# A two-layer diffusion backbone in fp32 on one core: another hand-written order for its first stage

## Chip, cores and metric

The kernel runs on one core of one Trainium2 chip. The metric is device time in microseconds, the median of several executions; lower is better. Input layouts are prepared on the host and are not timed.

## What is computed

Two layers work on 256 context tokens and 256 latent tokens of width 1024. Each layer is a SwiGLU FFN (width 2816), a token mixer, and a second FFN, all wrapped in RMS norms whose shift, scale and gate come from a conditioning vector (one vector for the latent tokens, one for the context). For the change only the first FFN's entry counts:

```
mod_l = silu(c) @ w_mod[l] + b_mod[l]        # 9 vectors of 1024; mod_c from c_ctx
h  = rms_norm(x, norm_pre) * (1 + scale) + shift
g, u = split(h @ w_in, 2)
x  = x + 0.5 * gate * rms_norm((silu(g) * u) @ w_out, norm_post)
```

## The kernel before

Activations lie transposed: `x` is 128 partitions by 8 tiles of 128 channels by 512 tokens (context, then latent). Every product of the FFN is made of three fp32r products: weights and activations are each split into a rounded part (`hi`, `hh`) and a rest (`lo`, `hl`), and hi·hh, hi·hl and lo·hh are summed. `split` (line 168) makes the parts of a weight in two halves, the cast on ScalarE (L173), the subtraction on VectorE (L174); a weight unit is one 512 KB load into one of 4 staging buffers (`raw`), giving 128 output columns.

The first stage has a long chain of its own: `hh` and `hl` for a pair of channel tiles need the RMS statistics of all of `x`, and the shift and scale of that pair. Shift and scale are a quarter of a small matrix product: `quarter_load` (L977) brings 2 MB of `w_mod` in 8 loads, `quarter_rows` (four fp32 products of 512 columns each, in four 32-row strips of one bank, issued as 8 instructions) multiplies them with `cs` = silu(c), `quarter_end` copies the rows on ScalarE (L989), transposes them back with small products (tile `pc`) and finishes the vectors on VectorE (L203, L206). The rest of the modulation is not made this way but by `mod_tile`, which sums on VectorE (L196) against `cb`, a broadcast silu(c); these sums run as a stream beside other work.

Inside `first_units` (L1040 and on) the order of SP (which issues the loads), TensorE, VectorE and ScalarE is written by hand: each engine executes its part of the steps in the order of the string `STEPS` (L63). The letters, with a number n:

- `x`: load pair n of `x`. `a`: squares of pair n on ScalarE (L1055, L1058), chained adds on VectorE (L1059). `t`: statistics: products with ones on TensorE, scaling on VectorE (L1069), power -1/2 on GpSimd (L241). `y`: transpose and broadcast of the norm (L1080), copied to SBUF as `rb` by ScalarE (L1081).
- `c`: silu of the conditioning into `cs` (L1018) and the selector `pick` (L1020).
- `q`, `r`, `s`, `f`: loads, first rows, second rows and end of quarter n; quarter n gives the vectors of pair n.
- `u`: load of unit n. `w`: its split.
- `h`: pair n of `hh` and `hl`: scaling by `rb` on VectorE (L1086), `hh` by ScalarE (L1091), the unrounded copy by VectorE for the pair's first tile (L1095) and by ScalarE for its second (L1093), the difference `hl` on VectorE (L1097).
- `*n`: all products that are possible for channel tiles k < n, in the order of k first and unit second. A unit's products keep one PSUM bank over all k.
- `d`, `e`: load and silu of `cb`. `z`, `l`: constants of the mixer.

Six units (0 to 5) go through this stage, 144 products of 512 columns; unit 6 and all after it go through the ordinary path, in which loads, splits and products are ordered by a planner. `product` (L1046) issues the three products of one unit and channel tile:

```
hi, lo = got["w%d" % u]
for j, (w, h) in enumerate(((hi, hh), (hi, hl), (lo, hh))):
    pe.matmul(bank[u], lhsT=w[:, k, :], rhs=h[:, k, :], ...)
```

All matmuls that go through the helper `Products.matmul` stand at L113 in the profile.

Of the kernel before, what the change touches and what calls it, by code (L numbers as in the profile page):

```python
# [8 lines left out]
F32 = mybir.dt.float32  # L9
# [3 lines left out]
OP = mybir.AluOpType  # L13

P = 128
D = 1024
KT = D // P
SEQ = 256
T = 2 * SEQ
# [40 lines left out]

STEPS = ("x1 x3 a1 x0 x2 u1 a3 u0 c0 a0 q0 q1 a2 w0 t0 r0 w1 y0 s0 f0 u2 u4 u3 r1 h0 q2 s1 u5 *2 w2 *2 w4 f1 *2 w3 *2 h1 "  # L63
         "r2 s2 *3 q3 f2 *4 r3 w5 h2 d0 z0 s3 *2 f3 e0 h3 *3 l0 *8")
F_ACT = "vavavava"
MANUAL0 = {mybir.EngineType.SP, mybir.EngineType.PE, mybir.EngineType.DVE, mybir.EngineType.Activation}

# [14 lines left out]
def backbone(ctx: ExitStack, tc: tile.TileContext, xT, vecs, crow, w_mod, w_in, w_out, w_mi, w_mo, w_lru, w_cm, b_cm, lam, w_last, out):  # L82
    nc = tc.nc
    ve, sc, gp, te = nc.vector, nc.scalar, nc.gpsimd, nc.tensor
# [4 lines left out]
    hp = ctx.enter_context(tc.tile_pool(name="hp", bufs=3))  # L89
# [6 lines left out]
    def nm(s):  # L96
        cnt[0] += 1
        return f"{s}_{cnt[0]}"

    def tt_(dt=F32, shape=(P, T)):  # L100
        return tp.tile(list(shape), dt, tag="t", name=nm("t"), bufs=NT)

    def pbank():
        return ps.tile([P, 512], F32, tag="mm", name=nm("mm"))
# [26 lines left out]
    vec = const.tile([P, NVEC], F32, name="vec")  # L131
    nc.sync.dma_start(vec, vecs)
    x = const.tile([P, KT, T], F32, name="x")
    hh = const.tile([P, KT, T], F32R, name="hh")
    hl = const.tile([P, KT, T], F32R, name="hl")

    def V(name, i, n=1):
        o = _OFF[name] + i
        return vec[:, o:o + n]

    ident = const.tile([P, P], F32, name="ident")
# [93 lines left out]
    def mcol(l, v, m, s):  # L235
        return modv[l][:, v, m, s:s + 1]


    def rsqrt(ms, n):
        v = sp.tile([P, n], F32, tag="rs", name=nm("rs"), bufs=4)  # L240
        gp.tensor_tensor(v, ms, power[:, :n], op=OP.pow)  # L241
        return v
# [762 lines left out]
    def halves_sum(v, m, raws):  # L1005
        sums = sp.tile([P, 2, 2], F32, tag="sums", name=nm("sums"), bufs=2)
        for h in range(2):
            for s in range(2):
                ve.scalar_tensor_tensor(junk[:, 0:512], raws[h], 1.0, cb[:, s, 512 * h:512 * h + 512],
                                        op0=OP.mult, op1=OP.mult, accum_out=sums[:, h, s:s + 1])  # L1010
        part = modv[0][:, v, m, :]
        ve.scalar_tensor_tensor(part, sums[:, 0], V("b_mod", v * KT + m), sums[:, 1], op0=OP.add, op1=OP.add)
        if v == 1:
            ve.tensor_scalar(part, part, 1.0, V("norm_pre", m), op0=OP.add, op1=OP.mult)
# [25 lines left out]
    def first_units(evac):  # L1040
        got, bank = {}, {}
        units = 1 + max(int(e[1]) for e in STEPS.split() if e[0] == "u")
        todo = [(k, u) for k in range(KT) for u in range(units)]
        acc, rb = tt_(), tt_()

        def product(k, u):  # L1046
            if k == 0:
                bank[u] = pbank()
            hi, lo = got["w%d" % u]
            for j, (w, h) in enumerate(((hi, hh), (hi, hl), (lo, hh))):  # L1050
                pe.matmul(bank[u], lhsT=w[:, k, :], rhs=h[:, k, :], start=(k == 0 and j == 0), stop=(k == KT - 1 and j == 2))

        def squares(m):
            if not summed:
                sc.activation(acc, x[:, m], AF.Square)  # L1055
            else:
                sq = tt_()
                sc.activation(sq, x[:, m], AF.Square)  # L1058
                ve.tensor_tensor(acc, acc, sq, op=OP.add)  # L1059
            summed.append(m)  # L1060

        summed, dgs = [], []

        def statistics():
            st = ps_st.tile([P, 4, 2], F32, tag="st", name=nm("st"))
            for tt in range(4):
                pe.matmul(st[:, tt, :], lhsT=acc[:, tt * P:(tt + 1) * P], rhs=ones[:, 0:2], start=tt == 0, stop=tt == 3)
            ms0 = const.tile([P, 4], F32, name="ms0")
            ve.tensor_scalar(ms0, st[:, :, 0], 1.0 / D, EPS, op0=OP.mult, op1=OP.add)  # L1069
            r = rsqrt(ms0, 4)  # L1070
            for s in range(2):
                msq[s] = ms0[:, 2 * s:2 * s + 2]
                dgs.append(r[:, 2 * s:2 * s + 2])

        def scales():
            p = ps_st.tile([P, T], F32, tag="st", name=nm("rb"))
            for s in range(2):
                for tt in range(2):
                    a = SEGS[s][0] + tt * P
                    te.transpose(p[:, a:a + P], dgs[s][:, tt:tt + 1].to_broadcast([P, P]), ident)  # L1080
            sc.copy(rb, p)  # L1081

        def first_h(ms):
            tmps = {m: hp.tile([P, T], F32, tag="sg", name=nm("tmp"), bufs=2) for m in ms}
            for m in ms:
                ve.tensor_tensor(tmps[m], x[:, m], rb, op=OP.mult)  # L1086
            for m in ms:
                for s in range(2):
                    a, b = SEGS[s]
                    A, B = mcol(0, 1, m, s), mcol(0, 0, m, s)  # L1090
                    sc.activation(hh[:, m, a:b], tmps[m][:, a:b], AF.Identity, scale=A, bias=B)  # L1091
                    if F_ACT[m] == "a":
                        sc.activation(tmps[m][:, a:b], tmps[m][:, a:b], AF.Identity, scale=A, bias=B)  # L1093
                    else:
                        ve.tensor_scalar(tmps[m][:, a:b], tmps[m][:, a:b], A, B, op0=OP.mult, op1=OP.add)  # L1095
            for m in ms:
                ve.tensor_tensor(hl[:, m], tmps[m], hh[:, m].bitcast(F32), op=OP.subtract)  # L1097

        raws = {}

        for what in STEPS.split():
            c, n = what[0], int(what[1])
            got[what] = True
            if c == "x":
                nc.sync.dma_start(x[:, 2 * n:2 * n + 2], xT[:, 2 * n:2 * n + 2])
            elif c == "a":
                for m in (2 * n, 2 * n + 1):
                    squares(m)
            elif c == "t":
                statistics()  # L1110
            elif c == "y":
                scales()
            elif c == "c":
                conditioning()
            elif c == "d":
                for s in range(2):
                    row = crow[:, s]
                    nc.sync.dma_start(cb[:, s], bass.AP(tensor=row.tensor, offset=row.offset, ap=[[0, P], [1, D]]))
            elif c == "e":
                for s in range(2):  # L1120
                    sc.activation(cb[:, s], cb[:, s], AF.Silu)
            elif c == "u":
                raws[what] = wp.tile([P, KT, P], F32, tag="raw", name=nm("raw"), bufs=NRAW)
                nc.sync.dma_start(raws[what], w_in[0, 0, n])
            elif c == "w":
                got[what] = [wp.tile([P, KT, P], F32R, tag=t, name=nm(t), bufs=NSPL) for t in ("hi", "lo")]
                for a in (0, 4):
                    split(raws["u%d" % n][:, a:a + 4], *(t[:, a:a + 4] for t in got[what]))
            elif c == "q":
                quarter_load(n)  # L1130
            elif c == "r":
                quarter_rows(n, 0)
            elif c == "s":
                quarter_rows(n, 4)
            elif c == "f":
                quarter_end(n)
            elif c in "vb":
                raws[what] = halves_load("bv".index(c), n)
            elif c in "VB":
                halves_sum("BV".index(c), n, raws[what.lower()])  # L1140
            elif c == "h":
                first_h((2 * n, 2 * n + 1))
            elif c == "z":
                mixer_consts(0)
                nc.sync.dma_start(lamt, lam)
            elif c == "l":
                decays()
            else:
                for k, u in list(todo):
                    if k < n and "h%d" % (k // 2) in got and "w%d" % u in got and (k - 1, u) not in todo:  # L1150
                        todo.remove((k, u))
                        product(k, u)
        assert not todo
        for j in range(units // 2):
            evac(j, bank[2 * j], bank[2 * j + 1], 0, T)
        return units // 2
# [24 lines left out]
def _layout(i):  # L1181
# [18 lines left out]
    w_mod = np.ascontiguousarray(wm.transpose(0, 2, 3, 4, 1)).reshape(L, 9, KT, P, D)  # L1200
    for q in (int(e[1]) for e in STEPS.split() if e[0] == "q"):
        rows = wm[0, :, 1::-1, 2 * q:2 * q + 2].reshape(2, 2, 2, P, 512).transpose(0, 1, 3, 2, 4)
# [38 lines left out]
```

## Time and profile before

| | us |
|---|---|
| median of 3 runs | 1646.81 (1646.08 to 1649.19) |
| the profiled execution, its time | 1645.51 |
| the profiled execution, its span | 1643.7 |

The profile is one execution. Times are microseconds from the span's start unless marked ns. PE is TensorE, PEld its weight loads, DVE VectorE, ACT ScalarE, POOL GpSimd, SPq the queue of the engine that issues the loads. A row names the line, the engine, the operation, and output <- input by the program's names; xN counts instructions that stand merged in one row. The chain of waits is followed back from the last instruction, at each step to what released it. Matmuls overlap, so their durations add up to more than the distance between their starts.

### The profile page before, as it was taken

To read this page: it belongs to the slowest core of one execution; us is meant where nothing else is said; L and a number is where in the kernel's file an instruction comes from. 1 tells how busy PE (TensorE), PEld (TensorE's weight loads), DVE (VectorE), ACT (ScalarE), POOL (GpSimd) and SP (SyncE) were. 2 spreads that over 40 slices of the span, in tenths; PEclk is the share of its full clock that TensorE was granted. 3 is DMA by queue.
4 is the path that set the end of the run, shared out by engine and by line. 5 is a ranking of instruction groups with operands and counts; after the bars stand their busy time and mean duration, and the time that the engine had idled before them with its cause. 6 is when DMAs were issued, how large, how long until landed. Compare 5 with 4: busy or idle time off the path is not lost.

```text
span 1643.7 us, 23402 instructions
## 1 busy us (share of the span) xinstructions
PE 1614.8 (98%) x8832; PEld 1372.6 (84%) x8832; DVE 1165.1 (71%) x2183; ACT 735.8 (45%) x1378; POOL 120.0 (7%) x166
## 2 busy tenths in 40 slices
PE   6999999999999999999999999999999999999998
PEld 3788888889977998888888998888888998789997
DVE  4799898548789777866763887767432888875554
ACT  5523322244697662332233562322222579764543
POOL 0000000005000500000000410000000410000000
PEclk9999999999999999999999999999999999989999
DMA  9568677431323225655542226655422316145552
GB/s 372 181 218 258 204 234 225 142 120 48 103 71 119 78 96 186 219 166 170 183 160 87 93 66 193 222 161 171 136 92 88 103 64 217 53 137 196 181 192 78
DMA packets 73906, 249.97 MB, mean 152 GB/s; under 512 B 8384, under 2 KB 10048, under 8 KB 73792
## 3 DMA queue, kind: packets, MB, share of 16 engines
q1 hardware_dynamic: 73216, 247.94, 46.0%
q8 instruction: 69, 1.13, 0.3%
q10 hardware_dynamic: 576, 0.52, 0.1%
q14 instruction: 45, 0.37, 0.1%
HBM read 247.39 MB, written 1.05 MB: 151 GB/s over the span
## 4 chain that ended last, share of the span: by engine, by line
PE 89%; DVE 6%; ACT 3%; issue 1%; DMA 1%; POOL 0%; SPq 0%; POOLq 0%; DVEq 0%; ACTq 0%
PE mm L113 87%; PE st L113 1%; DVE x L271 1%; PE mod L113 1%; DVE sq L394 1%; DVE t L703 0%; DVE z L270 0%; DVE tmp L262 0%; ACT hi L173 0%; DMA x<-in_xT 0%; DVE t L397 0%; POOL rs L241 0%; DVE lo L174 0%; PE pc L113 0%; DVE t L332 0%
## 5 line engine op out<-in xcount | busy, mean ns | idle before, releaser
L173 ACT CAST hi<-raw 128x512 fp32r<-128x512 f32 (+1 forms) x596 | 343.3, 610 | 673.3 <-PE mm L113 476.2
L113 PE MATMUL mm<-hh,hi 128*128 128x512 f32 (+1 forms) x1840 | 627.0, 349 | 1.2 <-ACT hh L263 1.1
L113 PE MATMUL mm<-hl,hi 128*128 128x512 f32 (+1 forms) x1840 | 623.7, 346 | 0.5 <-DVE hl L256 0.5
L174 DVE TENSOR_TENSOR lo<-raw,hi 128x512 fp32r<-128x512 f32 (+1 forms) x596 | 387.2, 679 | 156.1 <-ACT hi L173 153.0
L113 PE MATMUL mm<-hh,lo 128*128 128x512 f32 (+1 forms) x1840 | 467.8, 346 | 0.0
L113 PEld LDWEIGHTS mm<-hh,hi 128*128 128x128 f32 x1840 | 346.9, 189 | 53.7 <-ACT hh L1091 3.3
L113 PEld LDWEIGHTS mm<-hl,hi 128*128 128x128 f32 x1840 | 347.1, 189 | 49.3 <-issue 1.2
L196 DVE SCALAR_TENSOR_TENSOR junk<-raw,cb 128x1024 bf16<-128x1024 f32 x256 | 312.8, 1222 | 77.2 <-DMA raw<-in_w_mod 73.7
L113 PEld LDWEIGHTS mm<-hh,lo 128*128 128x128 f32 x1840 | 326.1, 189 | 47.3
L113 PE MATMUL mm<-t,hi 128*128 128x512 f32 (+1 forms) x1056 | 240.6, 367 | 0.0
L113 PEld LDWEIGHTS mm<-t,hi 128*128 128x128 f32 x1056 | 182.8, 188 | 35.7 <-issue 0.2
L397 POOL TENSOR_TENSOR t<-t,sq 128x256 f32<-128x256 f32 x112 | 94.1, 855 | 712.3 <-ACT sq L391 702.4
L113 PE MATMUL mm<-t,lo 128*128 128x512 f32 (+1 forms) x528 | 131.5, 367 | 0.0
L113 PEld LDWEIGHTS mm<-t,lo 128*128 128x128 f32 x528 | 92.5, 188 | 17.7
L480 DVE TENSOR_TENSOR sg<-sg,mm 128x512 f32<-128x512 f32 (+1 forms) x72 | 45.9, 639 | 76.7 <-PE mm L113 76.7
L113 PE MATMUL mm<-t,hh 128*128 128x256 f32 x512 | 71.2, 281 | 0.0
L113 PEld LDWEIGHTS mm<-t,hh 128*128 128x128 f32 x512 | 65.7, 188 | 0.5
L173 ACT CAST t<-sg 128x512 fp32r<-128x512 f32 (+1 forms) x94 | 50.6, 541 | 34.3 <-DVE sg L480 31.2
L174 DVE TENSOR_TENSOR t<-sg,t 128x512 fp32r<-128x512 f32 (+1 forms) x94 | 55.2, 588 | 1.1 <-ACT t L173 1.1
L113 PE MATMUL mm<-hi,t 128*128 128x512 f32 x176 | 55.1, 394 | 0.0
L332 DVE TENSOR_TENSOR t<-t,mm 128x256 f32<-128x256 f32 (+1 forms) x66 | 35.4, 536 | 27.3 <-PE mm L113 27.1
L263 ACT ACTIVATE hh<-tmp,modv 128x256 fp32r<-128x256 f32 x72 | 42.4, 596 | 23.6 <-DVE tmp L262 23.3
(177 smaller groups left out, 1209.1 us busy)
## 6 DMA issues: line engine op xcount, KB each, us to landing
raw<-in_w_in SPq DMA_DIRECT2D x176, 512.0 KB, 3.5
raw<-in_w_mod SPq DMA_DIRECT2D x128, 512.0 KB, 4.2
raw<-in_w_out SPq DMA_DIRECT2D x48, 512.0 KB, 3.3
raw<-in_w_mi SPq DMA_DIRECT2D x36, 512.0 KB, 4.1
raw<-in_w_last SPq DMA_DIRECT2D x22, 512.0 KB, 3.3
raw<-in_w_out SPq DMA_DIRECT2D x24, 384.0 KB, 3.7
t<-in_w_mod SPq DMA_DIRECT2D x32, 256.0 KB, 5.8
raw<-in_w_mo SPq DMA_DIRECT2D x8, 512.0 KB, 3.9
```

Of the source, the lines that this page charges most:

```text
L113: te.matmul(dst, lhsT=lhsT, rhs=rhs, start=start, stop=stop)
L173: sc.copy(hi, src)
L174: ve.tensor_tensor(lo, src, hi.bitcast(F32), op=OP.subtract)
L196: ve.scalar_tensor_tensor(junk, raw.rearrange("p k c -> p (k c)"), 1.0, cb[:, s], op0=OP.mult, op1=OP.mult, accum_out=modv[l][:, v, m, s:s ...
L263: sc.activation(hh[:, m, a:b], tmp, AF.Identity, scale=A, bias=B)
L271: ve.scalar_tensor_tensor(x[:, m, a:b], z, mcol(l, 3 * i + 2, m, s), x[:, m, a:b], op0=OP.mult, op1=OP.add)
L332: ve.tensor_tensor(y[m][:, a:b], y[m][:, a:b], p[:, :b - a], op=OP.add)
L394: ve.scalar_tensor_tensor(q[2], y, G, x[:, m, a:b], op0=OP.mult, op1=OP.mult)
L397: (gp if JACC[c] == "g" else ve).tensor_tensor(acc[c], acc[c], q[c], op=OP.add)
L480: ve.tensor_tensor(sg[:, :b - a], sg[:, :b - a], pu[:, :b - a], op=OP.mult)
```

## The change

The string of steps is replaced. `c0` comes first. All of quarter 0 is loaded ahead of the units, then units 1, 0, 2 and 4, quarter 1 and unit 3. A new step `n` (`first_n`) takes the scaling by `rb` out of `h`; it is called before `h` of the same pair. A new step `k` (`fill`) issues n fp32 products of 128x128 by 256 columns into a bank that nobody reads: `k2` ahead of `f0`, `k4` behind it, `k2` ahead of `f1`. The split of unit 0 comes after `h0`. Products of units 0, 1, 2 and 4 with the first pair come ahead of the rows of quarter 1; the rows of quarters 2 and 3 come one step of k apart. Within one product group the order is hi·hh, lo·hh, hi·hl. Everything behind the first six units is written as before.

```diff
--- before.py
+++ after.py
@@ -60,8 +60,9 @@
 
 
 
-STEPS = ("x1 x3 a1 x0 x2 u1 a3 u0 c0 a0 q0 q1 a2 w0 t0 r0 w1 y0 s0 f0 u2 u4 u3 r1 h0 q2 s1 u5 *2 w2 *2 w4 f1 *2 w3 *2 h1 "
-         "r2 s2 *3 q3 f2 *4 r3 w5 h2 d0 z0 s3 *2 f3 e0 h3 *3 l0 *8")
+
+STEPS = ("c0 x1 x3 x0 x2 q0 u1 u0 u2 u4 q1 u3 a1 a3 a0 a2 t0 r0 y0 n0 s0 k2 f0 k4 w1 h0 w0 *2 w2 *2 w4 *2 r1 s1 k2 f1 w3 n1 *2 h1 "
+         "q2 u5 *3 r2 s2 *4 f2 w5 n2 h2 q3 *5 r3 s3 d0 *6 f3 n3 z0 h3 e0 l0 *8")
 F_ACT = "vavavava"
 MANUAL0 = {mybir.EngineType.SP, mybir.EngineType.PE, mybir.EngineType.DVE, mybir.EngineType.Activation}
 
@@ -1047,7 +1048,7 @@
             if k == 0:
                 bank[u] = pbank()
             hi, lo = got["w%d" % u]
-            for j, (w, h) in enumerate(((hi, hh), (hi, hl), (lo, hh))):
+            for j, (w, h) in enumerate(((hi, hh), (lo, hh), (hi, hl))):
                 pe.matmul(bank[u], lhsT=w[:, k, :], rhs=h[:, k, :], start=(k == 0 and j == 0), stop=(k == KT - 1 and j == 2))
 
         def squares(m):
@@ -1080,10 +1081,20 @@
                     te.transpose(p[:, a:a + P], dgs[s][:, tt:tt + 1].to_broadcast([P, P]), ident)
             sc.copy(rb, p)
 
+        tmps = {}
+
+        def first_n(ms):
+            for m in ms:
+                tmps[m] = hp.tile([P, T], F32, tag="sg", name=nm("tmp"), bufs=2)
+                ve.tensor_tensor(tmps[m], x[:, m], rb, op=OP.mult)
+
+        def fill(n):
+
+            p = pbank()
+            for _ in range(n):
+                te.matmul(p[:, :SEQ], lhsT=ident, rhs=vec[:, :SEQ], start=True, stop=True)
+
         def first_h(ms):
-            tmps = {m: hp.tile([P, T], F32, tag="sg", name=nm("tmp"), bufs=2) for m in ms}
-            for m in ms:
-                ve.tensor_tensor(tmps[m], x[:, m], rb, op=OP.mult)
             for m in ms:
                 for s in range(2):
                     a, b = SEGS[s]
@@ -1138,6 +1149,10 @@
                 raws[what] = halves_load("bv".index(c), n)
             elif c in "VB":
                 halves_sum("BV".index(c), n, raws[what.lower()])
+            elif c == "n":
+                first_n((2 * n, 2 * n + 1))
+            elif c == "k":
+                fill(n)
             elif c == "h":
                 first_h((2 * n, 2 * n + 1))
             elif c == "z":
@@ -1145,7 +1160,7 @@
                 nc.sync.dma_start(lamt, lam)
             elif c == "l":
                 decays()
-            else:
+            elif c == "*":
                 for k, u in list(todo):
                     if k < n and "h%d" % (k // 2) in got and "w%d" % u in got and (k - 1, u) not in todo:
                         todo.remove((k, u))
```

## Rows read from the trace of the kernel before

**Rows 1.** The page, part 1: busy us, share of the span, instructions

```profile
PE 1614.8 (98%) x8832; PEld 1372.6 (84%) x8832; DVE 1165.1 (71%) x2183; ACT 735.8 (45%) x1378; POOL 120.0 (7%) x166
```

**Rows 2.** The chain of waits, 0 to 100 us: start, duration, what

```profile
8.91 1.28 ACT L1018
...
10.20 0.22 ACT cs L1018
...
10.97 0.70 DVE t L1059
...
13.36 0.70 DVE t L1059
...
14.10 1.87 PE st L113 x8
...
18.88 1.99 PE mod L113 x8
...
20.89 0.59 ACT t L989
...
21.53 1.87 PE pc L113 x8
23.40 3.57 PE mod L113 x16
26.97 5.07 PE mm L113 x18
...
35.73 1.85 PE mod L113 x16
...
49.90 50.28 PE mm L113 x215
```

**Rows 3.** The timeline of TensorE: start, duration, instruction

```profile
26.90 0.80 PE L113 MATMUL mm<-hh,hi 128*128 128x512 f32 x1
...
31.88 0.95 PE L113 MATMUL pc<-pick,t 128*128 128x2 f32 x8
...
48.95 0.95 PE L113 MATMUL pc<-pick,t 128*128 128x2 f32 x8
...
68.05 0.40 PE L113 MATMUL mm<-hh,hi 128*128 128x512 f32 x1
```

**Rows 4.** The timeline of ScalarE: start, duration, instruction, idle before

```profile
27.76 2.17 ACT L173 CAST hi<-raw 128x512 fp32r<-128x512 f32 x4
...
35.14 1.58 ACT L1091 ACTIVATE hh<-tmp,modv 128x256 fp32r<-128x256 f32 x3 [3.69 <-DVE tmp L1086]
...
51.00 1.59 ACT L1091 ACTIVATE hh<-tmp,modv 128x256 fp32r<-128x256 f32 x3 [0.84 <-DVE tmp L1086]
```

**Rows 5.** The timeline of VectorE: start, duration, instruction, idle before

```profile
33.13 0.16 DVE L206 SCALAR_TENSOR_TENSOR modv<-modv,vec 128x4 f32<-128x4 f32 x1
33.21 1.29 DVE L174 TENSOR_TENSOR lo<-raw,hi 128x512 fp32r<-128x512 f32 x2
...
36.72 0.69 DVE L1097 TENSOR_TENSOR hl<-tmp,hh 128x512 fp32r<-128x512 f32 x1
...
52.57 0.69 DVE L1097 TENSOR_TENSOR hl<-tmp,hh 128x512 fp32r<-128x512 f32 x1
...
54.38 0.69 DVE L1097 TENSOR_TENSOR hl<-tmp,hh 128x512 fp32r<-128x512 f32 x1
```

**Rows 6.** Tile x up to 16 us; and a window with granted clock, DMA share, GB/s

```profile
L1105 SPq DMA_DIRECT2D x<-in_xT x4: 415/428/432, 1.2 to 2.6; - x4
...
DMA to landing us min/median/max: 3.7/6.5/7.9
...
26.00:28.00 2.00, 2.00 (x11) 0.91 (x4) 0.85 (x3) 1.93 (x5) 0.00 (x0) 1.00 1.05 404
```

**Rows 7.** The groups of 0 to 80 us; and a window's busy time by engine

```profile
L196 DVE SCALAR_TENSOR_TENSOR junk<-raw,cb 128x1024 bf16<-128x1024 f32 x6 | 7.3, 1220 | 0.0
...
60.00:100.00 40.00, 40.00 (x173) 32.22 (x172) 37.81 (x79) 16.07 (x32) 0.32 (x1) 1.00 0.62 202
```

## The prediction

> **What bounds the kernel now.** I read the page first: TensorE is busy for 1614.8 of 1643.7 us [rows 1]. So time is saved or lost where TensorE waits, and half of its 28.9 idle us lie ahead of its first instruction at 14.10. Then I read the chain of the first 100 us: the rows to see are the second activation-table load (1.28 us) with the Silu behind it, four chained adds of squares (10.97 to 14.06), the statistics at 14.10, the two halves of the first modulation quarter (r0, s0) up to 20.87, the copy of its rows, and the transposing products (pc) that end at 23.40 [rows 2]. From the first unit product at 26.90 TensorE never stops: the 144 products of the six first units, two more quarters (16 row products each, 1.85 us) and three pc groups fill 26.90 to 68.05, where unit 6 begins [rows 2, 3]. Of these 41.15 us, 0.77 us are a slow start: the first 18 products take 4.98 us up to pc f1 at 31.88, while later ones come every 50.28/215 = 0.234 us, 4.21 for 18 [rows 2, 3].
>
> Last, what follows a pc group on the other engines, because the new order leans on it. After pc f1 (ends 32.83) VectorE finishes the vectors at 33.29, makes a unit's two lo halves (33.21; one takes 0.69, so the first ends 33.90) and scales x; ScalarE starts hh at 35.14, and VectorE has hl at 37.41 [rows 3 to 5]. That is 1.07 us to the first lo half, 2.31 to the start of hh, so 3.45 to a product that reads both halves of hh (two instructions, about 1.1 us), and 4.6 to one that reads hl. After pc f3 (ends 49.90) no lo halves stand in between: hh starts 1.10 us later, hl is there after 3.36 (53.26) [rows 3 to 5]. In the kernel before none of this costs anything, since 12 products and a row quarter, or many products, stand behind each pc.
>
> **The change, part by part.** Times count from the span's start; T is the end of the first pc group.
>
> *Silu first.* One table load and the Silu leave ScalarE's way (1.50 us at 8.91 to 10.42) [rows 2]. Then x decides: its last quarter is issued at 2.6 and lands at most 7.9 later, 10.5 [rows 6]. Two squares and the last two chained adds (0.70 each, 0.80 apart) end at about 12.75, so the statistics start at 12.8, 1.3 us earlier. If x's last quarter is not the one that takes 7.9 us, it may be 1.8.
>
> *Modulation weights behind x.* q0 now lands before u1 and u0, and its halves are read in order behind the statistics, as before. x, q0, u1 and u0 are the same 5 MB as before, all in use by 18.88, and at about 404 GB/s [rows 6] u2 and u4 follow by 21.5 and q1 by 26.7; u3 waits on SP for u1's staging buffer (about T+1.8), with q2, u5 and q3 queued behind it, all needed 10 us or more after they land. I cost the transfers at nothing; every use below is later.
>
> *x scaled ahead.* For the first pair the two scalings run between the first rows copy and pc; hh can start when the vectors are done, T+0.5, instead of 1.1 after. For pairs 1 to 3 the scaling stands behind the vectors on VectorE as before (f1 w3 n1, f2 w5 n2, f3 n3): nothing won.
>
> *Fills.* s0 ends at 20.87 - 1.3 = 19.57, the rows are copied by 20.2. Two unread fp32 products of 256 columns stand before pc. Eight row instructions do four 512-column products side by side in 1.99 us at the start and 0.93 us later (16 in 1.85) [rows 2]; half a column count gives about 1.0 us a fill at the slow pace and 0.46 at the quick one. So pc starts between 20.5 and 21.6 and takes 1.87 or 0.95 us [rows 2, 3]: T lies between 21.45 and 23.4. Before, TensorE worked from 14.10 to 20.87 without a pause and pc was still slow [rows 2], which speaks for 23.4; the fills are fuller work than narrow products, which speaks for 21.45; I take the middle, T = 22.5, 0.9 us ahead of 23.40. The Trainium skill, "TensorE: Matmul & The Clock Gate", section "What's actually happening", says that the clock is held back by default and that activity releases it. If the fills count as that, T is 21.45 and the sum below +9.0; if they do not, +11.0; no row here has a fill. The four fills behind pc end by T+4.0 at the latest and delay nothing. The two before f1 cost 0.93, half of it instead of a copy wait.
>
> *The first products, TensorE's order.* The products go column tile by column tile, unit 0 first, and w0 is now behind h0. ScalarE does six hh instructions (3.38 us, 51.00 to 54.38 [rows 4, 5]) from T+0.5, then casts w0's first half (0.6, [rows 4]): the first product starts at **T+4.45**. It now reads lo second; VectorE reaches w0's lo only behind hl: 0.56 us more. Before, the distance was 3.5 us, and r1 s1 ran in it; they now come later and cost 1.85 us in the open.
>
> *The waits behind each pc.* f1: one product, wait 1.0 for w3's lo; five products; hh at +3.45, wait 1.2; hl, wait 0.7: 2.9 us. f2: 1.0 for w5's lo, then eleven products cover hh, 0.5 for hl: 1.5. f3: all products with k up to 5 are issued ahead of it, so nothing covers it: 2.4 for hh, 0.7 for hl: 3.1. With the first 0.56 this is 8.06 us.
>
> *Hi-lo order and the modulation stream.* Same products, same loads of weights: nothing in the steady pace. The Silu of cb now comes after h3, at about 72, so the six modulation sums that VectorE did around 53 to 62 (7.3 us, [rows 7]) move into a stretch where it is busy 37.81 of 40 us. Their results are wanted only near the end of the first FFN and TensorE did not wait there, so zero, with 5 us as the upper bound.
>
> **Sum.** Content of TensorE from the first product: 41.15 - 0.77 + 1.85 + 0.93 = 43.16. Unit 6 starts at T + 4.45 + 43.16 + 8.06 = T + 55.67 = 78.17, against 68.05: **+10.1 us**. What follows is the same work, bound by TensorE, and shifts along. The profiled execution took 1645.51 us for its span of 1643.7 and becomes 1655.6; it stood 1.3 below the median, so I predict 1656.9. From T alone the sum goes from +9.0 to +11.0; a slow first burst like the one before adds 0.8.
>
> **The rivals.**
> *The clock falls in the new waits.* The granted clock reads 1.00 (the 2.4 GHz level) from 26 to 28 [rows 6] though the products there still ran slow; the quick pace came only among the first 18 products, after unbroken work from 23.40, with 3.57 - 1.85 = 1.72 us lost on r1 s1 and 0.77 on the products [rows 2], 2.5 in all. With waits at T+4, f1 and f3 it could fall again. For: r1, s1 and pc ran slow after pauses of under 1 us. Against: those pauses came before it was ever quick. Two falls at that price cost 5 us: 1662. The Trainium skill, "TensorE: Matmul & The Clock Gate", section "What's actually happening", has the slow state come back with idleness; by that rule this rival holds, with its 1662, if waits of 1 to 3 us are idle enough. No row here shows a fall.
>
> *TensorE does not wait, because the written order is not what it executes.* If ready products of u1, u2 and u4 went ahead, the first would start at T+1.65, when hh's first tile is whole, and the 8.06 us would vanish: unit 6 at T + 44.8 = 67.3, or 66.2 at the quick T, so 0.7 to 1.8 us faster, 1645.5; with the clock quick from r0 on (T near 19.7) 3.5 us faster. It decides below 5 us of waits in all, out of 12.5. Against: before, 18 products precede pc f1 [rows 2], exactly as its steps are written.
>
> *Silu first does nothing,* if Square needs a table of its own. Before, Squares follow the Silu with no load between [rows 2], so hardly; it would add 1.3 us: 1658.2.
>
> **How the numbers follow.** Forecast 0.72, alone 1654.5 to 1659.5; clock 0.12; no waits 0.09; Silu idle 0.02; some 0.05 that the rest of the schedule, laid anew behind this start, takes back half. 1651 to 1663 leaves out the no-wait case and the worst of the clock case. A measurement can tell 0.2%, 3.3 us, from no change. Faster takes the quick end of the no-wait case, 0.04; the same its rest and a part of the half case, 0.09; slower 0.87.
>
> **What would show it.** Statistics at 12.8; one table load ahead of x; the first unit product 4 to 5 us behind the first pc with ScalarE's w0 cast as releaser; waits of TensorE on lo and hh behind f1, f2 and f3, the longest at f3; unit 6 near 78. Wrong if the first product starts before 24, if f3 is covered, or if unit 6 starts before 72.

## The result, and the profile after

| | before | after |
|---|---|---|
| median of 4 runs each, us | 1647.66 (1646.08 to 1649.19) | 1666.99 (1666.27 to 1669.34) |
| ratio, with its 95% interval | | 1.0123 (1.0109 to 1.0137) |
| the profiled execution, time / span, us | 1645.51 / 1643.7 | 1667.14 / 1665.4 |

Slower, as forecast, but by 19.3 us instead of 10.1: 4.0 us beyond the upper end of the range. On the page TensorE is busy longer, for 1626.4 us against 1614.8 [rows 1], although the changed kernel has only 16 instructions more (the fills): some of its products ran slower. The page of after, part 1:

```profile
PE 1626.4 (98%) x8848; PEld 1381.8 (83%) x8848; DVE 1165.8 (70%) x2183; ACT 735.5 (44%) x1377; POOL 119.7 (7%) x166
```

**The first stage on TensorE.** The timeline of TensorE in after (start, duration, instruction; in brackets the idle time before it and what ended that). One line is added ahead of them, so L113, L174 and L480 of the kernel before are L114, L175 and L481 here; the fills stand at L1095.

```profile
13.55 1.86 PE L114 MATMUL st<-ones,t 128*128 128x2 f32 x8 [13.55 <-DVE t L1060]
...
20.12 1.17 PE L1095 MATMUL mm<-vec,ident 128*128 128x256 f32 x4
21.13 0.95 PE L114 MATMUL pc<-pick,t 128*128 128x2 f32 x8
21.94 1.97 PE L1095 MATMUL mm<-vec,ident 128*128 128x256 f32 x8
26.48 0.49 PE L114 MATMUL mm<-hh,hi 128*128 128x512 f32 x1 [2.57 <-ACT hi L174]
27.30 0.79 PE L114 MATMUL mm<-hh,lo 128*128 128x512 f32 x1 [0.33 <-DVE lo L175]
27.89 0.63 PE L114 MATMUL mm<-hl,hi 128*128 128x512 f32 x1
28.32 0.63 PE L114 MATMUL mm<-hh,hi 128*128 128x512 f32 x1
...
30.70 0.39 PE L114 MATMUL mm<-hh,hi 128*128 128x512 f32 x1
...
39.19 0.50 PE L114 MATMUL mm<-hh,lo 128*128 128x512 f32 x1 [0.79 <-DVE lo L175]
...
41.52 0.49 PE L114 MATMUL mm<-hh,hi 128*128 128x512 f32 x1 [0.90 <-ACT hh L1102]
...
42.69 0.50 PE L114 MATMUL mm<-hl,hi 128*128 128x512 f32 x1 [0.44 <-DVE hl L1108]
...
67.05 0.95 PE L114 MATMUL pc<-pick,t 128*128 128x2 f32 x8
70.24 0.50 PE L114 MATMUL mm<-hh,hi 128*128 128x512 f32 x1 [2.25 <-ACT hh L1102]
...
71.42 0.79 PE L114 MATMUL mm<-hl,hi 128*128 128x512 f32 x1 [0.44 <-DVE hl L1108]
72.01 0.63 PE L114 MATMUL mm<-hh,hi 128*128 128x512 f32 x1
...
74.93 0.39 PE L114 MATMUL mm<-hh,lo 128*128 128x512 f32 x1
...
81.00 0.40 PE L114 MATMUL mm<-hh,hi 128*128 128x512 f32 x1
...
89.87 0.47 PE L114 MATMUL mm<-hh,hi 128*128 128x512 f32 x1 [3.11 <-DVE sg L481]
```

Three things are to be seen. The waits on lo, hh and hl stand where the prediction put them: behind the first pc, pc f1 and pc f3 (the pair behind f2, 0.79 and 0.22, is not shown). Twice, from 27.30 and from 71.42, products start 0.43 us apart instead of 0.234, until 30.70 and 74.93. And unit 6 starts at 81.00, 12.95 later than the 68.05 of [rows 3]; behind it, at 89.87, comes a wait for VectorE's product L481 that the kernel before does not have. The windows of after, with the granted clock in the third column from the right, show what the 0.43 is:

```profile
28.00:30.00 2.00, 2.00 (x6) 1.54 (x5) 2.00 (x4) 1.03 (x2) 0.00 (x0) 0.50 1.05 393
...
72.00:74.00 2.00, 2.00 (x6) 1.60 (x5) 1.49 (x4) 2.00 (x3) 0.39 (x1) 0.50 0.00 0
...
1340.00:1360.00 20.00, 19.77 (x152) 19.42 (x152) 16.42 (x45) 10.16 (x22) 4.44 (x6) 0.91 0.16 53
```

At 28 and at 72 the clock is granted at 0.50, the 1.2 GHz level, right behind the two longest waits of the stage. Eight steps from 27.30 to 30.70 take 3.40 us where 8 x 0.234 = 1.87 would do: 1.5 us lost; the eight from 71.42 to 74.93 lose 1.6, 3.2 together.

**The wait at unit 7.** The chain of waits of after, from the load to the multiplication that lets TensorE go on:

```profile
82.81 4.75 DMA raw<-in_w_in
...
87.63 0.63 ACT hi L174
...
88.28 0.57 DVE lo L175
...
88.89 0.17 DVE s L1038
...
89.13 0.60 DVE sg L481
```

The PSUM bank (the memory in which a unit's products are summed) that unit 7 needs is that of unit 1, and it comes free when VectorE has multiplied unit 1's result (L481). (Some expectations below call this unit 8.) On VectorE that multiplication stands behind the last steps of `l0` (L1038), with lo halves of later units between them, and one of those halves waits for a load that was issued late, at 82.81. It is the third of the four that the queue of loads (SP) shows from 78.80 on; the queue of after, and then of before:

```profile
44.73 9.62 SPq L195 DMA_DIRECT2D raw<-in_w_mod  x2
78.80 5.57 SPq L180 DMA_DIRECT2D raw<-in_w_in  x4
```

```profile
43.59 0.95 SPq L194 DMA_DIRECT2D raw<-in_w_mod  x2
...
56.32 13.49 SPq L179 DMA_DIRECT2D raw<-in_w_in  x4
```

Two of the four staging buffers hold weights of the modulation stream in both kernels. Before, the second of its sums on VectorE ends at 56.29 and the next load goes out at 56.32:

```profile
55.07 1.22 DVE L196 SCALAR_TENSOR_TENSOR junk<-raw,cb 128x1024 bf16<-128x1024 f32 x1
```

After, the sums wait for `cb`'s Silu on ScalarE, which now comes behind `h3`, and the load waits with them:

```profile
72.35 1.99 ACT L1132 ACTIVATE cb<-cb 128x1024 f32<-128x1024 f32 x2
```

```profile
77.45 0.17 DVE L1028 TENSOR_SCALAR lt<-lt 128x16 f32<-128x16 f32 x1 [2.79 <-POOL lt L1027]
77.54 1.22 DVE L197 SCALAR_TENSOR_TENSOR junk<-raw,cb 128x1024 bf16<-128x1024 f32 x1
```

The Silu is not all of it: it is over at 74.34 and the first sum at 74.65, but the second sum stands behind L1028, the step of `l0` that waits for GpSimd. Before, the second sum came ahead of that wait. After, it ends at 78.76, the load is issued at 78.80, 22.5 us later than before, and the wait at 89.87 puts TensorE 16.3 us behind instead of 12.95.

**Behind it.** From 90 to 950 us the distance between the two profiles stays within 16.1 and 16.4 us, the n-th instruction of TensorE against the n-th, counted from the end. Late in the execution of after three more stretches of lower clock (960 to 980, 1340 to 1360 above, 1440 to 1480 against a smaller one before) make it 21.7.

### The profile page after: what moved, and what is told of

It is laid out like the page before. It is cut to its first block, busy times and chain, and to the rows that moved or that the text cites. A ratio compares the mean times of both kernels' runs of the same rounds, so it can differ in the third digit from the quotient of the medians.

```text
span 1665.4 us, 23428 instructions
## 1 busy us (share of the span) xinstructions
PE 1626.4 (98%) x8848; PEld 1381.8 (83%) x8848; DVE 1165.8 (70%) x2183; ACT 735.5 (44%) x1377; POOL 119.7 (7%) x166
## 4 chain that ended last, share of the span: by engine, by line
PE 88%; DVE 5%; ACT 1%; issue 1%; POOL 0%; DMA 0%; POOLq 0%; DVEq 0%; ACTq 0%
PE mm L114 86%; PE st L114 1%; DVE x L272 1%; DVE sq L395 1%; DVE z L271 0%; DVE tmp L263 0%; DVE t L398 0%; DVE lo L175 0%; POOL rs L242 0%; DMA raw<-in_w_in 0%; DVE t L333 0%; DVE hl L257 0%; DVE ms L418 0%; PE rb L249 0%; DVE t L733 0%
## 5 line engine op out<-in xcount | busy, mean ns | idle before, releaser
L114 PE MATMUL mm<-hh,hi 128*128 128x512 f32 (+1 forms) x1840 | 629.8, 350 | 10.0 <-ACT hh L1102 3.1
L174 ACT CAST hi<-raw 128x512 fp32r<-128x512 f32 (+1 forms) x596 | 343.1, 610 | 668.3 <-PE mm L114 473.2
L114 PE MATMUL mm<-hl,hi 128*128 128x512 f32 (+1 forms) x1840 | 626.9, 348 | 1.6 <-DVE hl L1108 1.1
L175 DVE TENSOR_TENSOR lo<-raw,hi 128x512 fp32r<-128x512 f32 (+1 forms) x596 | 388.1, 680 | 159.5 <-ACT hi L174 156.3
L114 PE MATMUL mm<-hh,lo 128*128 128x512 f32 (+1 forms) x1840 | 470.8, 348 | 1.9 <-DVE lo L175 1.9
L114 PEld LDWEIGHTS mm<-hh,hi 128*128 128x128 f32 x1840 | 349.2, 190 | 61.8 <-ACT hi L174 6.5
L114 PEld LDWEIGHTS mm<-hl,hi 128*128 128x128 f32 x1840 | 349.7, 190 | 52.0 <-DVE hl L1108 2.4
L114 PEld LDWEIGHTS mm<-hh,lo 128*128 128x128 f32 x1840 | 328.7, 190 | 50.1 <-DVE lo L175 2.8
L114 PE MATMUL mm<-t,hi 128*128 128x512 f32 (+1 forms) x1056 | 240.1, 367 | 0.0
L114 PEld LDWEIGHTS mm<-t,hi 128*128 128x128 f32 x1056 | 182.9, 188 | 35.3 <-issue 0.2
L114 PE MATMUL mm<-t,lo 128*128 128x512 f32 (+1 forms) x528 | 131.6, 367 | 0.0
L114 PEld LDWEIGHTS mm<-t,lo 128*128 128x128 f32 x528 | 92.5, 188 | 17.9
L481 DVE TENSOR_TENSOR sg<-sg,mm 128x512 f32<-128x512 f32 (+1 forms) x72 | 45.9, 640 | 82.9 <-PE mm L114 82.7
L114 PE MATMUL mm<-t,hh 128*128 128x256 f32 x512 | 71.5, 282 | 0.0
L114 PEld LDWEIGHTS mm<-t,hh 128*128 128x128 f32 x512 | 65.9, 188 | 0.5
L174 ACT CAST t<-sg 128x512 fp32r<-128x512 f32 (+1 forms) x94 | 50.6, 541 | 22.4 <-DVE sg L481 19.3
L175 DVE TENSOR_TENSOR t<-sg,t 128x512 fp32r<-128x512 f32 (+1 forms) x94 | 55.2, 588 | 0.5 <-ACT t L174 0.5
L114 PE MATMUL mm<-hi,t 128*128 128x512 f32 x176 | 55.3, 395 | 0.0
L480 ACT ACTIVATE sg<-mm 128x512 f32<-128x512 f32 (+1 forms) x72 | 40.1, 557 | 33.9 <-PE mm L114 33.4
```

Of the source, the lines that this page charges most:

```text
L114: te.matmul(dst, lhsT=lhsT, rhs=rhs, start=start, stop=stop)
L174: sc.copy(hi, src)
L175: ve.tensor_tensor(lo, src, hi.bitcast(F32), op=OP.subtract)
L480: sc.activation(sg[:, :b - a], pg[:, :b - a], AF.Silu)
L481: ve.tensor_tensor(sg[:, :b - a], sg[:, :b - a], pu[:, :b - a], op=OP.mult)
```

## The experiments

My theory after the result: the 16.3 us are the waits I had summed, two falls of the clock (3.2 us), and the modulation stream's late Silu (3.3 us); the late stretches are chance of the execution. Rivals: the late stretches come from the change; the new product order or Silu first cost something of their own; the fills are what keeps the clock. The diffs below show only the pieces of `STEPS` that differ.

**The two kernels again.** `b_again` and `a_again` are before and after unchanged.

> The kernel before, unchanged, to see how much of the 20 us belongs to the clock late in the kernel. After the change the two traces drift apart by 12.9 us up to unit 6, by 3.3 us at units 7 and 8, and by 5.4 us in three places behind 950 us where the granted clock falls. Theory A (those late falls are a matter of the single execution, not of the change): 1647.7 us, and the mean clock of its executions spreads from 0.986 to 0.995. Theory B (the change brings them, by shifting the work): 1647.7 us, every execution at 0.994 to 0.996, and in the profile only one stretch of slow clock between 1430 and 1455.

Measured 1647.09, ratio 1.0005 (0.9995 to 1.0016). The windows of b_again:

```profile
940.00:960.00 20.00, 19.80 (x153) 19.44 (x153) 17.34 (x45) 9.98 (x21) 6.46 (x9) 0.91 0.17 55
1320.00:1340.00 20.00, 19.82 (x153) 19.46 (x152) 16.61 (x45) 9.24 (x21) 5.29 (x9) 0.91 0.17 53
```

The stretches of lower clock near 950 and 1330 are there without any change; the profile of before just had neither. It was a quick one at the end, and a slow one at the start: the timeline of TensorE in b_again has its first product earlier,

```profile
24.95 0.51 PE L112 MATMUL mm<-hh,hi 128*128 128x512 f32 x1
25.65 0.50 PE L112 MATMUL mm<-hl,hi 128*128 128x512 f32 x1 [0.20 <-DVE hl L1096]
```

26.90 in [rows 3], and quick from the first product on; unit 6 starts at 66.29. Its pc, at 21.17, is quick too, with no fill ahead of it.

> The changed kernel, unchanged, in more executions. Between 130 us and 900 us its profile stood 16.2 us behind the one of before; the other 5.4 us came from stretches of slow clock behind 950 us, and the kernel before, executed again, shows such stretches too and spreads from 1643 to 1651 us. The order of instructions on every engine is the same in both kernels from 130 us on. Theory A (the late stretches belong to the execution): executions spread over 6 us and more, from 1661 to 1669, the mean clock from 0.985 to 0.993, the median falls to 1663 to 1665. Theory B (with the work moved by 16 us, the clock's rhythm always meets the late mixer in the bad way): 1666 to 1669 with the clock at 0.986 to 0.989, as in the first four.

Measured 1665.55, 1.0111 (1.0094 to 1.0127). Unit 6 at 81.23, the wait at unit 7 again, 16.7 us behind before's profile at 100 us and so 18.4 behind b_again's, beside medians that differ by 17.7 (in the runs of a_again) and 19.3 (in the first ones). These two profiles have the same late stretches of lower clock, and the 18.4 stays within 18.0 and 18.5 up to 1600 us. So the first stage, up to unit 7, carries nearly all of the difference; whether the change also makes the late stretches likelier stays open, 0 to 2 us of it.

**The modulation stream alone.** `a_e0`: `d0` and `e0` earlier.

```diff
-n2 h2 q3 *5 r3 s3 d0 *6 f3 n3 z0 h3 e0 l0 *8
+n2 h2 d0 q3 e0 *5 r3 s3 *6 f3 n3 z0 h3 l0 *8
```

> The changed kernel with the load of cb moved ahead of quarter 3 and its Silu ahead of the products up to k = 5, so that the modulation sums can run from about 60 us. Theory A (the modulation stream's two loads hold two of the four staging buffers until 78.8 and so delay unit 8): TensorE's wait of 3.1 us at 89.9 is gone, the third load of the ordinary path is issued before 70 instead of at 78.8. Two of the sums now stand between VectorE's steps behind pc f3, so the wait there may grow from 2.25 to 4.7 us: net 1663.7 to 1666. Rival (the loads are late because of their number, not of cb): the wait stays, 1667.

Measured 1666.76, 1.0125 (1.0110 to 1.0141). SP's queue and then the end of the stage on TensorE:

```profile
70.00 16.86 SPq L180 DMA_DIRECT2D raw<-in_w_in  x4
```

```profile
71.83 0.55 PE L114 MATMUL mm<-hh,hi 128*128 128x512 f32 x1 [3.27 <-ACT hh L1102]
...
74.85 0.79 PE L114 MATMUL mm<-hl,hi 128*128 128x512 f32 x1 [2.04 <-DVE hl L1108]
```

VectorE then multiplies unit 1's result, 7 us sooner than in after:

```profile
82.21 0.69 DVE L481 TENSOR_TENSOR sg<-sg,mm 128x512 f32<-128x512 f32 x1 [0.29 <-PE mm L114]
```

The load goes out 8.8 us sooner, and the wait at unit 7 is gone, as the theory wants. (That TensorE comes later is not the reason: it reaches unit 7 at 90.34, well behind the multiplication.) So moving the Silu and the sums removes the wait; a_best below has the wait although both are early. But nothing is won, since VectorE now does three sums between the vectors and `hl` of the last pair: the waits behind f3 are 5.31 us instead of 2.69, the clock stays low until 79.1, and unit 6 starts 16.7 us late instead of 12.95. In this order the sums delay `hl` instead of the load.

**One wait alone.** `a_u1` lets unit 1, whose parts are ready, go before `w0`:

```diff
-k4 w1 h0 w0 *2 w2
+k4 w1 h0 *2 w0 *2 w2
```

> The changed kernel with the products of unit 1 and the first pair ahead of unit 0's split: one product group more, none in all. Theory A (the first product waits for unit 0's cast on ScalarE, and the clock falls in that wait): first product at 23.7 instead of 26.5, clock quick throughout, unit 6 starts about 3.3 us earlier (77.7 instead of 81.0), 1663.7. Rival (the start is bound by hl and by unit 0 in any case): unit 6 at 80 or later, 1666 to 1667.

Measured 1663.06, 1.0099 (1.0081 to 1.0117). TensorE's timeline:

```profile
23.57 0.51 PE L114 MATMUL mm<-hh,hi 128*128 128x512 f32 x1
23.91 0.39 PE L114 MATMUL mm<-hh,lo 128*128 128x512 f32 x1
25.03 0.50 PE L114 MATMUL mm<-hl,hi 128*128 128x512 f32 x1 [0.73 <-DVE hl L1108]
...
86.60 0.48 PE L114 MATMUL mm<-hh,hi 128*128 128x512 f32 x1 [2.95 <-DVE sg L481]
```

The wait of 2.57 is gone (0.73 and 0.56 for `hl` come in its place), the products between are quick at once, the clock does not fall before 68.2; unit 6 comes 3.1 us sooner than in after, while the wait at unit 7 stays. `a_f3` moves `f3` ahead of the products of the last k that it had behind it:

```diff
-d0 *6 f3 n3
+d0 f3 *6 n3
```

> The changed kernel with the end of quarter 3 (its pc group) ahead of the 18 products of k = 5, which then cover what follows it. Theory A: the wait of 2.25 us for hh and of 0.44 for hl behind pc f3 and the slow clock behind them (1.4 us) go, a wait of 0.8 us for the rows copy comes ahead of pc: unit 6 at 77.7 instead of 81.0, 1663.7. Rival (the wait only moves to another place, for instance to unit 6, whose split is late): unit 6 earlier but 1666 to 1667.

Measured 1661.13, 1.0092 (1.0074 to 1.0109). Waits and low clock behind f3 are gone, unit 6 comes 4.9 us sooner than in after; 0.9 of that is there at the first product (25.61), ahead of the edit, and belongs to the execution. Then, on TensorE:

```profile
85.82 0.47 PE L114 MATMUL mm<-hh,hi 128*128 128x512 f32 x1 [4.01 <-DVE sg L481]
...
87.07 0.63 PE L114 MATMUL mm<-hl,hi 128*128 128x512 f32 x1
```

The wait at unit 7 grows from 3.11 to 4.01 and the clock falls behind it, so 2.4 of the 4.9 us are given back: of 4.9 us that unit 6 gained, unit 1's multiplication on VectorE gained only 4.05. The wait's end hangs on VectorE's chain, not on when TensorE is ready: L1028 waits for GpSimd until 72.98, then come the sums and lo halves, the load issued at 78.22 and unit 1's multiplication at 85.00.

**All three.** `a_fix` joins the edits of a_u1, a_f3 and a_e0.

> The changed kernel with all three edits together: products of unit 1 ahead of unit 0's split, quarter 3's end ahead of the products of k = 5, cb and its Silu earlier. Alone, the first two brought unit 6 forward by 3.1 and 4.9 us, the third took away the wait of 3.3 us at unit 8 and put two sums into the chain behind f3, now covered by 18 products. Theory A (the three are separate causes): unit 6 at about 73 (81.0 - 8.0), no wait of TensorE above 1 us at units 7 and 8, and 11 us less than the changed kernel: 1655 to 1657. What stays (some 5 us in the first stage) are the waits behind f1 and f2, r1 s1 in the open and the fills. Rival (they cover one another): unit 6 at 75 or later, or a wait at unit 8 of 2 us and more; 1659 or more.

Measured 1659.86 (1654.44 to 1663.23), 1.0079 (1.0058 to 1.0100). The theory's 11 us show up to unit 7 but not in the time, which is the rival's. In its profile unit 6 starts at 73.64, 5.6 us behind before's, no wait at unit 7, no fall of the clock until 423. Still two waits at 112 and 113 us follow (1.02 and 0.60, for ScalarE's and VectorE's split of unit results): 7.8 us behind at 126. So the waits of the stage, the clock in them and the stream make up 10.6 of 16.3 us at unit 7, of which 2.1 come back as these two waits. The fall at 423 costs another 1.6; b_lo2 below, the kernel before but for one order, has such a fall at 414. The rest is what the theory left in place: the content in the open (r1 and s1 1.85, the fills 0.93) and the waits that a_fix keeps. That there is no wait at unit 7 is a near thing: unit 1's multiplication ends at 79.14 and unit 7 starts at 79.29.

**The fills.** `a_nofill` leaves out the unread products alone (`k2`, `k4`, `k2`).

> The changed kernel without the three groups of unread products. In its trace the granted clock rises at 20.5, within the first of them, and pc runs quick; the wait for unit 0's cast behind them lets it fall again. Theory A (the fills buy the quick pc and lose it in their own length): pc starts at 20.4 instead of 21.1 and runs slow (1.87), ends at 22.3 instead of 22.1, the first product starts at 26.7 instead of 26.5 and the products up to about 30 run slow as they do now; ahead of f1 nothing is lost. Unit 6 within 0.7 us of 81.0, total within 2 us of 1667. Rival (the fills lengthen TensorE's path): unit 6 at 79.5 or earlier, 1665. Third (they shorten it): unit 6 at 82.5 or later.

Measured 1667.54, 1.0130 (1.0112 to 1.0148). TensorE's timeline, then two windows:

```profile
20.31 1.05 PE L114 MATMUL pc<-pick,t 128*128 128x2 f32 x8 [0.79 <-ACT t L990]
25.77 0.80 PE L114 MATMUL mm<-hh,hi 128*128 128x512 f32 x1 [4.40 <-ACT hi L174]
```

```profile
26.00:30.00 4.00, 3.98 (x9) 2.82 (x10) 3.54 (x6) 2.32 (x5) 0.00 (x0) 0.50 1.04 397
...
42.00:46.00 4.00, 4.00 (x10) 2.74 (x10) 1.74 (x3) 2.09 (x4) 0.00 (x0) 0.50 0.91 317
```

pc is quick without a fill ahead of it, so it does not need the fills. Behind the wait, now 4.40 long, the clock is low until 32.3, again behind f1 (39.2 to 46.0) and behind f3: unit 6 starts at 82.71, 1.7 later. By these profiles the clock is up longer with the fills, and they pay about what they cost; between the medians of this kernel and after (1667.54, 1666.99) nothing can be told.

**Parts put into the kernel before.** `b_silu` puts `c0` first and changes nothing else. `b_lo2` takes only the order hi·hh, lo·hh, hi·hl:

```diff
-((hi, hh), (hi, hl), (lo, hh))
+((hi, hh), (lo, hh), (hi, hl))
```

> The kernel before with one step moved: the conditioning's Silu first. In the changed kernel the statistics started at 13.55 instead of 14.10, with seven chained adds of squares in a row from 8.83 on. Theory A (behind the removed table load stands VectorE's chain of adds, 0.8 us each, not the landing of x): statistics at 13.5 to 13.6, 0.5 us earlier than 14.10; unit 6 at most 0.6 us earlier, total the same within the 0.2% that can be told. Rival (my prediction's term: only x's last landing stands behind it): statistics at 12.8.

Measured 1647.20, 1.0000 (0.9991 to 1.0009). TensorE's timeline:

```profile
15.54 3.85 PE L113 MATMUL mod<-t,cs 128*32 128x512 f32 x8
```

The statistics start at 13.73 (14.10 in [rows 2]), but the first rows then take 3.85 us instead of 1.86: they wait for their loads. What Silu first gives is lost to q0's landing unless that is moved as well.

> The kernel before with the product order of the change alone: hi by hh, lo by hh, hi by hl. Theory A (nothing waits for a lo or an hl there): unit 6 within 0.3 us of where the executions of before have it, given the same start, total within 0.2% of before. Rival (the order changes the pace of the weight loads): the distance of products away from 0.234 us, 144 times; even 0.01 us would be 1.4 us at unit 6.

Measured 1646.61, 0.9997 (0.9985 to 1.0009): the order itself costs nothing; the pace stays 0.234.

`b_best` is before with Silu first, x scaled ahead and two fills before f0, and the order of units untouched:

```diff
-x1 x3 a1 x0 x2 u1 a3 u0 c0 a0 q0 q1 a2 w0 t0 r0 w1 y0 s0 f0
+c0 x1 x3 a1 x0 x2 u1 a3 u0 a0 q0 q1 a2 w0 t0 r0 w1 y0 n0 s0 k2 f0
```

> The kernel before with those parts of the change that can run beside other work: Silu first, the first pair's scaling ahead of the vectors, two unread products between s0 and the first pc group. Its order of loads, units and products stays. Theory A (the fills close the gap ahead of pc, so that the clock is quick for pc, r1, s1 and the first products; up to 0.9 + 1.7 + 0.8 us): unit 6 at 64.5 to 66.5 instead of 68.05, total 1643.5 to 1645.5, faster by 0.1 to 0.2%. Rival (quarter 1's rows then wait for their loads, or the clock rises no sooner): unit 6 at 67 or later, total within 1 us of before.

Measured 1646.71, 1.0001 (0.9992 to 1.0011). What the change's early steps give is swallowed by the loads: the rows at 15.36 take 3.85 us and those of quarter 1 3.11.

**The changed order, mended.** `a_best` keeps the new loads, lets unit 1 go first, moves f1, r3, s3 and f3 ahead of products that can cover them and cb's Silu (`e0`) ahead of `h3`, drops the fills ahead of the first pc and of f1, and runs others (`k2`, and `j` on x) ahead of the statistics:

```diff
-k4 w1 h0 w0 *2 w2 *2 w4 *2 r1 s1 k2 f1 w3 n1 *2 h1
-q2 u5 *3 r2 s2 *4 f2 w5 n2 h2 q3 *5 r3 s3 d0 *6 f3 n3 z0 h3 e0 l0 *8
+k3 w1 h0 *2 w0 *2 w2 *2 w4 r1 s1 f1 *2 w3 *2 n1 h1
+q2 u5 q3 *3 r2 s2 *4 f2 r3 s3 w5 n2 h2 d0 *5 f3 e0 *6 n3 z0 h3 l0 *8
```

> An order that keeps the change's loads and its early units and mends what the runs found: unit 1's products ahead of unit 0's split, f1 with twelve products behind it, quarter 3's rows behind f2, f3 ahead of the products of k = 5, cb's Silu ahead of h3; fills moved to the time ahead of the statistics, on each pair of x as it lands, so that the clock is quick when the statistics come; three fills behind pc, none ahead of it and none before f1. Theory A (the first 22 us are bound by TensorE at the slow clock): first pc group ends at 18.5 to 20 instead of 22.1, first product at 20 to 21.5, unit 6 at 64 to 66.5, total 1642 to 1645, faster than before by 0.1 to 0.25%. Rival (the clock stays slow in spite of the fills, or falls in the pause behind pc): pc ends at 21.5 or later, unit 6 at 68 or later, total as before or slower.

Measured 1655.67 (1653.19 to 1659.00), 1.0053 (1.0040 to 1.0067): 11 us better than after, but slower than before and than the 1642 to 1645 expected. Unit 6 starts at 68.60, 0.55 behind [rows 3] and 2.3 behind b_again. TensorE's timeline from there:

```profile
78.05 0.47 PE L114 MATMUL mm<-hh,hi 128*128 128x512 f32 x1 [3.68 <-DVE sg L481]
...
79.14 0.63 PE L114 MATMUL mm<-hh,hi 128*128 128x512 f32 x1
```

The wait for unit 1's bank and a fall of the clock behind it are nearly all that is left of the loss up to 100 us: 6.0 us. Here the late Silu is not the cause: cb's Silu is over at 54.29 and three of the four sums at 63.74. Nor is a load: the third ordinary one goes out at 62.51, 6.2 us later than before, and in a_fix it goes out later still, at 66.66, without a wait. The chain of waits has no load in it, since ScalarE's cast waits for products of TensorE:

```profile
74.15 0.63 ACT hi L174
...
77.32 0.60 DVE sg L481
```

What the kernels with the wait share, as I read them, is VectorE's order: L481 stands behind `l0`, and lo halves of later units come between the steps of `l0` from L1028 on. There are eleven of them here and nine in after (with three sums), six in a_fix, none in a_e0 and none in before, where `l0` is over at 64.51 and unit 0's result comes at 65.03. No run moves `l0` or L481, so this reading is not proved. No version here beats the kernel before.

## Why the prediction was right in direction and short in size

Two terms that I put at nothing failed: the clock ("Against: those pauses came before it was ever quick"), 3.2 us, and the modulation stream ("so zero"), 3.3 us. The waits that I had summed came nearly as written. What is left of the 19.3 us, some 3, is a matter of executions: I hung the sum on one of them, and up to 2 us stay open.

**Statistics, "1.3 us earlier": 0.5.** They start at 13.55. I let x's last quarter land at 10.5 and counted two squares and two adds behind it. From 8.17 on no square waits for x, and VectorE's own chain decides, as its timeline in after shows: six adds without a gap, 0.8 us apart, against four in [rows 2].

```profile
8.83 4.67 DVE L1060 TENSOR_TENSOR t<-t,t 128x512 f32<-128x512 f32 x6 [1.91 <-ACT t L1059]
```

Before, that chain stood idle for 0.94 us ahead of 10.97, so the Silu cost it less than its 1.50. Executions differ by as much as the gain: the statistics start at 14.10 and 14.60 in before and b_again, at 13.55 and 13.99 in after and a_again.

**T = 22.5: 22.08.** That this is so near is in part luck: the statistics came 0.75 later than I took them, and from there it went quicker, since pc ran in 0.95 and the two fills in 1.0 together, the quick end of my two bounds. The rule of the Trainium skill that I set beside it ("TensorE: Matmul & The Clock Gate", "What's actually happening") gave the right end; but a_nofill and b_again have pc quick without any fill, so the fills were not needed for it. The slow pc that I argued from is a trait of the one profile of before: b_again has T at 22.22, so against it the early steps gain 0.14 us and not 1.3.

**First product at T + 4.45: T + 4.40,** released by ScalarE's cast of w0, as written. **The waits, 8.06 us:** from 26.48 to 81.00 there are 54.52 us; without the content of 43.16 and the clock's 3.2, 8.2 are left. f1, f2 and f3 show the releasers that I named, f3 the longest. That rules out the rival that the written order is not executed. The one that the Silu does nothing falls too: after's Squares follow the Silu (4.48) with no table load between.

**The clock: the rival I gave 0.12 held.** "Against: those pauses came before it was ever quick" was the first step that failed: once quick, the clock did fall at 27.30 and 71.42, after idle times of 2.57 and 2.25 us, though not behind f1 and f2, with single waits up to 0.90, nor behind the 3.11 at unit 7. Its price was too high, 2.5 a fall; measured 1.5 and 1.6. By that section of the Trainium skill the slow state comes back with idleness. The trace agrees at the two falls, and a_u1, where the 2.57 us are gone and the first fall with them, shows it by experiment; the 3.11 us at unit 7 show that not every long wait does it.

**The modulation stream, "so zero, with 5 us as the upper bound": 3.3 us.** This was the second. I asked who reads the sums' results (nobody soon) and not what the sums hold while they wait: two of four staging buffers, and places in VectorE's order ahead of L481. The chain from there is load, split, L481, the PSUM bank, unit 7. a_e0 takes the wait away by moving the Silu and the sums. That they are the whole cause is not shown: a_best keeps a wait of 3.68 with the Silu early.

**The sum.** Unit 6: 78.17 - 0.42 (T) - 0.05 + 3.2 (clock) + 0.1 (waits and rest) = 81.00; unit 7 adds 3.3: 16.3 instead of 10.1. **"What follows shifts along"** fails at unit 7, where VectorE's order is another than before (it is the same again from 195 us on, TensorE's from 123 us), and holds behind it. But I hung the sum on one execution. Its start was 1.75 us slower than that of b_again, and its end quicker; a forecast of a difference that begins in the first 30 us should have allowed for that, up to 2 us more.

## What to carry to other kernels

When a background stream is delayed, price what it holds (buffers, banks, places in an engine's order), not only when its results are read. A wait put into a saturated TensorE stage costs its length and, for most of those of 2 us and more here, another 1.5 us or more of low clock; letting ready work go first (one `*2` in a_u1) saved both. Set a sum against several executions of the kernel before, since here two executions of the same code were 1.75 us apart at unit 6, and all executions of before spread from 1643 to 1651 us.

## What was not expected of the hardware

- The same kernel gets the quick clock at different points: in before the first three products still start 0.43 us or more apart, from 26.90 to 28.34 [rows 3], in b_again products are quick from 24.95 on, with the same work ahead of them. The granted clock reads 1.00 there in before too [rows 6]: in these profiles the column tells of the slow level only after it has first been quick.
- How long a wait is does not say whether the clock falls behind it: it fell behind 2.25 (after) and 4.01 us (a_f3), and in a_nofill at 39.2, behind a wait of 0.78 and within one of 0.79, but not in after behind 3.11 at unit 7, or behind 0.79, 0.90 and 0.44 at f1. What decides is not settled here.
- An unread fp32 product of 128x128 by 256 columns takes 0.49 us at the quick pace (four in 1.97), as much as two of the 512-column products of the FFN, whose starts lie 0.234 apart.
